# Eight of the 22 rows of blocks of a feed-forward's down product as seven products of sums, in the four feed-forwards of the second block

## The chip, the cores and the metric

The kernel runs on one core of a Trainium2 chip. The metric is the device time of one launch in microseconds; the median of three runs of the kernel before is 1603.33 us (1603.21 to 1605.09).

## The reference

Two transformer blocks over 256 tokens of width 1024, in float32. The first has a feed-forward, a mixer (neighbourhood attention and pooling), a second feed-forward and a gated embedding. The second block has six layers, and four of them are the feed-forwards that matter here:

```
def swiglu_2(x, w_in, w_out):
    gate, up = jnp.split(x @ w_in, 2, axis=-1)        # 1024 -> 2 x 2816
    return (jax.nn.silu(gate) * up) @ w_out           # 2816 -> 1024

for i in range(2):
    h = layer_norm(ALPHA * h + 0.5 * swiglu_2(h, ffn_w_in[i, 0], ffn_w_out[i, 0]), ...)
    h = layer_norm(ALPHA * h + mixer(h), ...)         # i = 0: gated linear attention, i = 1: retention
    h = layer_norm(ALPHA * h + 0.5 * swiglu_2(h, ffn_w_in[i, 1], ffn_w_out[i, 1]), ...)
```

Layer norms, attention and retention are unchanged by what follows, and so is the first block.

## The kernel before, in words

**Products.** All large products are done in a split form: each operand is a high part (rounded to the type fp32r) and a low part (the rest), and a product of blocks is three matmuls into the same PSUM bank, high by high, high by low, low by high (`mm3`, L215 to L219). The stationary operand is a block of 128 tokens by 128 rows of activations, the moving one 128 by 512 columns of weights. The 256 tokens are two token tiles.

**Weights** come in units of 128 x 2048 values (1 MB). `fetch` (L157) loads a unit into a `raw` buffer, ScalarE casts it to the high part `whi` (L174), and VectorE subtracts to get the low part `wlo` (L177). There are five buffers of each. The list `plan` holds the order of all units of the kernel; `unit` hands out the next one, and its argument `ahead` says how many units beyond it are to have been issued.

**Seven products for eight.** Where a weight matrix is taken as 2 x 2 blocks of 512 x 512 and the tokens as 2 x 2 blocks of 128 x 512, `seven` (L369) forms the four block products from seven products of sums (P1, P5, P7, P6, P3, P2, P4 in this order). Each has four block products (12 matmuls), a unit of weights of its own, made by `fetch_sum` (L182) from four raw units (L194 adds, L196 casts, L197 subtracts), and for P5, P7, P6 and P3 a sum of token blocks y1, y3, y2, y4, made by `sums_in` (L302). VectorE combines the results (L392 to L402). The kernel before does this for two of the six column chunks of gate and up in five feed-forwards, and for two pairs of chunks in the retention layer.

**A feed-forward** (`ffn`, L449) does the gate and up products chunk by chunk, multiplies silu(gate) by up (`finish`), transposes the result on TensorE and splits it into `hT[t, c]` for token tile t and chunk c. The down product (`lagged`, L406) then walks over 11 units of weights, each two rows of blocks (2 x 128 rows) by 1024 columns. For each unit `step(t, u)` does four block products (12 matmuls) into the two accumulators of token tile t; tile 1 follows tile 0 by three units, and the last two units of tile 1 are done one accumulator after the other. When tile 0 is finished, `after` adds it to the residual stream h and normalises it (`ln_post`, L329), and its transposes are put off by five and six ticks (`turn_in`); a tick is two block products. Tile 1's remaining steps run meanwhile.

**PSUM** buffers are eight, of one bank each: five with the tag `mm` (accumulators and products), three with the tag `tp` (transposes).

**Order.** The program is written as straight code with work put off by ticks (`defer`), but the order in each engine's queue is set when the kernel is built, by a list scheduler: of the instructions whose operands and buffers are expected to be there, the one written first goes first, and work written later is moved ahead if an engine would wait. Buffers of one tag are handed out in the order of the code. On the chip each queue then runs in the order written.

Of the kernel before, what the change touches and what calls it, by code (L numbers as in the profile page):

```python
# [11 lines left out]
F32 = mybir.dt.float32  # L12
# [20 lines left out]
LAG = 3  # L33
POOL_WINDOWS = (2, 4, 8, 16)
# [17 lines left out]
def ffn_units(g, u, d, seven=()):  # L52


    out = []
    for c in range(5):
        four = [(g, 2 * c), (g, 2 * c + 1), (u, 2 * c), (u, 2 * c + 1)]
        out += [(four, j) for j in range(7)] if c in seven else four
    return out + [(g, 10), (g, 11)] + [(d, i) for i in range(11)]
# [19 lines left out]
def all_units():  # L79
# [5 lines left out]
    p += ffn_units("s0g", "s0u", "s0d", SEVEN)  # L85
    p += chunk_units("gin", GLA_ORDER) + [("gout", i) for i in range(4)]
    p += ffn_units("s1g", "s1u", "s1d", SEVEN) + ffn_units("s2g", "s2u", "s2d", SEVEN)
    p += chunk_units("rin", RET_ORDER) + [("rout", i) for i in range(8)]
    return p + ffn_units("s3g", "s3u", "s3d", SEVEN)


class Build:
# [107 lines left out]
    def unit(self, name, i, kb, ahead=1):  # L200
# [3 lines left out]
        near = any(isinstance(p[0], list) for p in self.plan[self.taken:self.taken + 4])  # L204
# [200 lines left out]

    def lagged(self, x, name, n_units, after, lag=LAG, have=None, extra=None):  # L406


        lag = min(lag, n_units)
        late, self.late = self.late, None  # L410
        if late:
            self.defer(2, late)
# [18 lines left out]
        for i in range(n_units + lag):  # L431
            if i < n_units:
                w[i] = self.unit(name, i, 2, 0 if lag == n_units and i == lag - 1 else 1)
                step(0, i)
                if i == n_units - 1:
                    after(0, acc[0])
            if i >= lag and i - lag < n_units - 2:
                step(1, i - lag)
# [10 lines left out]
    def ffn(self, xT, r, wg, wu, wd, after, first=False, raws=None):  # L449
# [3 lines left out]
        def finish(c, t, ps_g, ps_u, n):  # L453
# [8 lines left out]
            if t == 0 and c:  # L462
                first_pr[c] = pr
            elif c:
                self.defer(4, lambda: turn(c, n, first_pr[c], pr))
            else:
                self.defer(4, lambda: hT.__setitem__((t, c), self.splitT(pr, n // P, "hT")))
# [15 lines left out]
        first_pr = {}  # L483

# [52 lines left out]
        self.lagged(lambda t, k: hT[t, k // 4][:, k % 4, :], wd, 11, after, have=lambda t, k: (t, k // 4) in hT)  # L537
# [471 lines left out]
    def run(self, ctx):  # L1009
# [89 lines left out]
        for i in range(6):  # L1099
            if i % 3 != 1:  # L1100
                f = 2 * (i // 3) + (i % 3) // 2
                body = lambda after: self.ffn(nx, None, f"s{f}g", f"s{f}u", f"s{f}d", after, raws=raws)
# [64 lines left out]
def layout(x, p, rpb, pool_w, pool_scale, w_in, w_br_attn, w_br_pool, w_out, ple_w_proj, ple_w_gate,  # L1167
# [21 lines left out]
    for i in range(2):  # L1189
        for j in range(2):  # L1190
            w = ffn_w_in_2[i, j]
            a[f"s{2 * i + j}g"], a[f"s{2 * i + j}u"] = units_ff(w[:, :DFF], w[:, DFF:])
            a[f"s{2 * i + j}d"] = units(ffn_w_out_2[i, j], 2, 1024)
# [27 lines left out]
```

## Time and profile before

| | |
|---|---|
| median of three runs | 1603.33 us |
| the profiled execution | 1602.33 us |
| its span, first to last instruction | 1600.5 us |
| TensorE busy | 1588.5 us, 99% |
| VectorE busy | 1189.7 us, 74% |
| ScalarE busy | 823.0 us, 51% |
| GpSimd busy | 102.5 us, 6% |
| granted TensorE clock, mean | 0.998 of full speed |
| moved by DMA | 308 MB, 192 GB/s |

The page groups instructions by line, engine, operation and operands; a row has their count, busy time, mean duration, and the idle time of the engine before them with what ended it. Matmuls are pipelined, so that one matmul's row shows 0.39 us, while the next one starts 0.23 us after it. In a timeline a line has the start in us from the span's start, the duration, engine, line of the kernel, operation, what it writes and reads, how many instructions were merged, and in brackets how long the engine stood idle before and what it waited for.

### The profile page before, as it was taken

To read this page: it belongs to the slowest core of one execution; us is meant where nothing else is said; L and a number is where in the kernel's file an instruction comes from. 1 tells how busy PE (TensorE), PEld (TensorE's weight loads), DVE (VectorE), ACT (ScalarE), POOL (GpSimd) and SP (SyncE) were. 2 spreads that over 40 slices of the span, in tenths; PEclk is the share of its full clock that TensorE was granted. 3 is DMA by queue.
4 is the path that set the end of the run, shared out by engine and by line. 5 is a ranking of instruction groups with operands and counts; after the bars stand their busy time and mean duration, and the time that the engine had idled before them with its cause. 6 is when DMAs were issued, how large, how long until landed. Compare 5 with 4: busy or idle time off the path is not lost. (4 is left out here: it accounts for less than half of the span.)

```text
span 1600.5 us, 18234 instructions
## 1 busy us (share of the span) xinstructions
PE 1588.5 (99%) x7377; PEld 1310.2 (82%) x7377; DVE 1189.7 (74%) x1050; ACT 823.0 (51%) x819; POOL 102.5 (6%) x102
## 2 busy tenths in 40 slices
PE   9999999999999999999999999999999999999998
PEld 7888888888888888888888888888888888888886
DVE  6654665568983789947648996699938899799954
ACT  7443554455562765634645553446624464456531
POOL 0000000000000100001012000100002401010000
PEclk9999999999999999999999999999999999999999
DMA  9764663543574555556534556545755543655550
GB/s 355 286 212 154 212 228 126 183 158 139 195 278 158 179 204 210 214 202 231 181 121 152 186 184 235 187 178 191 267 183 182 187 184 112 252 196 191 183 198 27
DMA packets 49796, 308.10 MB, mean 192 GB/s; under 512 B 6048, under 2 KB 7328, under 8 KB 15024
## 3 DMA queue, kind: packets, MB, share of 16 engines
q1 hardware_dynamic: 49568, 306.93, 53.1%
q8 instruction: 58, 0.95, 0.2%
q14 instruction: 26, 0.21, 0.0%
q10 hardware_dynamic: 144, 0.00, 0.0%
HBM read 305.86 MB, written 1.05 MB: 192 GB/s over the span
## 5 line engine op out<-in xcount | busy, mean ns | idle before, releaser
L177 DVE TENSOR_TENSOR wlo<-raw,whi 128x2048 fp32r<-128x2048 f32 (+1 forms) x239 | 520.2, 2184 | 273.8 <-ACT whi L174 273.8
L174 ACT CAST whi<-raw 128x2048 fp32r<-128x2048 f32 (+1 forms) x238 | 432.8, 1826 | 348.5 <-PE acc L219 190.5
L217 PE MATMUL mm<-whi,xTh 128*128 128x512 f32 x912 | 363.3, 398 | 0.2 <-ACT xTh L234 0.2
L219 PE MATMUL mm<-whi,xTl 128*128 128x512 f32 x912 | 356.3, 391 | 0.0
L218 PE MATMUL mm<-wlo,xTh 128*128 128x512 f32 x912 | 356.2, 391 | 0.0
L196 ACT CAST whi<-raw 128x2048 fp32r<-128x2048 f32 x84 | 160.3, 1910 | 104.7 <-DVE raw L194 66.7
L217 PE MATMUL acc<-whi,hTh 128*128 128x512 f32 x528 | 207.0, 392 | 0.0
L219 PE MATMUL acc<-whi,hTl 128*128 128x512 f32 x528 | 205.6, 389 | 0.0
L218 PE MATMUL acc<-wlo,hTh 128*128 128x512 f32 x528 | 205.5, 389 | 0.0
L219 PEld LDWEIGHTS mm<-whi,xTl 128*128 128x128 f32 x912 | 171.2, 188 | 37.7 <-DVE xTl L235 1.4
L217 PEld LDWEIGHTS mm<-whi,xTh 128*128 128x128 f32 x912 | 171.3, 188 | 35.7 <-issue 1.7
L218 PEld LDWEIGHTS mm<-wlo,xTh 128*128 128x128 f32 x912 | 171.5, 188 | 33.5
L197 DVE TENSOR_TENSOR wlo<-raw,whi 128x2048 fp32r<-128x2048 f32 x84 | 190.7, 2284 | 5.9 <-ACT whi L196 5.9
L219 PEld LDWEIGHTS acc<-whi,hTl 128*128 128x128 f32 x528 | 99.1, 188 | 21.0
L218 PEld LDWEIGHTS acc<-wlo,hTh 128*128 128x128 f32 x528 | 99.2, 188 | 20.1
L217 PEld LDWEIGHTS acc<-whi,hTh 128*128 128x128 f32 x528 | 99.1, 188 | 20.0
L194 DVE TENSOR_TENSOR raw<-raw 128x2048 f32<-128x2048 f32 x48 | 109.9, 2290 | 0.1
L217 PE MATMUL mm<-whi,xh 128*128 128x512 f32 x176 | 69.0, 394 | 0.7 <-ACT whi L174 0.4
L218 PE MATMUL mm<-wlo,xh 128*128 128x512 f32 x176 | 68.8, 391 | 0.0
L219 PE MATMUL mm<-whi,xl 128*128 128x512 f32 x176 | 68.6, 390 | 0.0
L234 ACT CAST hTh<-hT 128x512 fp32r<-128x512 f32 (+1 forms) x72 | 38.6, 546 | 56.0 <-PE hT L226 55.9
L341 POOL TENSOR_TENSOR rl<-mv,mhalf 128x1 f32<-128x1 f32 x12 | 11.7, 976 | 738.9 <-DVE mv L340 738.9
(259 smaller groups left out, 2027.4 us busy)
## 6 DMA issues: line engine op xcount, KB each, us to landing
raw<-in_rin SPq DMA_DIRECT2D x24, 1024.0 KB, 4.8
raw<-in_bin SPq DMA_DIRECT2D x16, 1024.0 KB, 4.8
raw<-in_f2g SPq DMA_DIRECT2D x12, 1024.0 KB, 4.8
raw<-in_s0g SPq DMA_DIRECT2D x12, 1024.0 KB, 4.7
raw<-in_gin SPq DMA_DIRECT2D x12, 1024.0 KB, 4.7
raw<-in_s1g SPq DMA_DIRECT2D x12, 1024.0 KB, 4.7
raw<-in_s2g SPq DMA_DIRECT2D x12, 1024.0 KB, 4.8
raw<-in_s3g SPq DMA_DIRECT2D x12, 1024.0 KB, 4.9
```

The lines of the kernel that those rows point to most:

```text
L174: nc.scalar.copy(hi[:, s], raw[:, s])
L177: nc.vector.tensor_tensor(out=lo[:, s], in0=raw[:, s], in1=hi[:, s].bitcast(F32), op=ALU.subtract)
L194: nc.vector.tensor_tensor(out=r[key], in0=r[key], in1=r[other], op=ALU.add)
L196: nc.scalar.copy(hi, r[key])
L197: nc.vector.tensor_tensor(out=lo, in0=r[key], in1=hi.bitcast(F32), op=ALU.subtract)
L217: mm(ps, x.hi, w.hi, start=start, stop=False)
L218: mm(ps, x.hi, w.lo, start=False, stop=False)
L219: mm(ps, x.lo, w.hi, start=False, stop=stop)
L234: self.nc.scalar.copy(hi, v)
L341: nc.gpsimd.tensor_tensor(out=r, in0=mv[:, 1:2], in1=self.mhalf[:, :1], op=ALU.pow)
```

## The change

In the four feed-forwards of the second block, the first eight rows of blocks of the down product (1024 x 1024 weights, chunks 0 and 1 of hT) are done as seven products of sums, the other 14 as before. A new list of units puts four of the ordinary units first (the lead, both token tiles at once), then the seven units of sums, then the remaining three. `seven_down` does the products: P6 in the fifth `mm` bank, the others in the three `tp` banks, since the accumulators hold four. Its combinations are not put together with the accumulators but added into h one by one (`into`). `pair_sums` makes the token sums: three blocks are put together again from high and low part and four differences formed on GpSimd, then split by ScalarE and VectorE; one block (`whole`) is kept unsplit. The loads of the next layer norm's gains, which use the buffers of y1 and y2, are issued after the seven products. On the host the first 1024 rows of the down weights are laid out as four 512 x 512 blocks.

```diff
--- before.py
+++ after.py
@@ -31,6 +31,7 @@
 ALPHA = 4 ** 0.25
 NEG = -3.0e38
 LAG = 3
+LEAD = 4
 POOL_WINDOWS = (2, 4, 8, 16)
 EDGE = 8
 SUMS = (("a", None), ("a", "b"), ("b", "c"), ("a", "c"), ("c", None), ("d", None), ("a", "d"))
@@ -49,14 +50,18 @@
         return Split(self.hi[i], self.lo[i])
 
 
-def ffn_units(g, u, d, seven=()):
+def ffn_units(g, u, d, seven=(), pair=False):
 
 
     out = []
     for c in range(5):
         four = [(g, 2 * c), (g, 2 * c + 1), (u, 2 * c), (u, 2 * c + 1)]
         out += [(four, j) for j in range(7)] if c in seven else four
-    return out + [(g, 10), (g, 11)] + [(d, i) for i in range(11)]
+    out += [(g, 10), (g, 11)]
+    if not pair:
+        return out + [(d, i) for i in range(11)]
+    return out + [(d, i) for i in range(4, 4 + LEAD)] + [([(d, i) for i in range(4)], j) for j in range(7)] + [(d, i) for i in range(4 + LEAD, 11)]
 
 
 def chunk_units(name, order):
@@ -82,11 +87,11 @@
     p += chunk_units("bin", MIX_ORDER) + [("bpl", 0), ("bat", 0), ("bpl", 1), ("bat", 1)] + [("bout", i) for i in range(4)]
     p += ffn_units("f2g", "f2u", "f2d", SEVEN)
     p += [("pgate", i) for i in range(4)] + [("pproj", 0)]
-    p += ffn_units("s0g", "s0u", "s0d", SEVEN)
+    p += ffn_units("s0g", "s0u", "s0d", SEVEN, True)
     p += chunk_units("gin", GLA_ORDER) + [("gout", i) for i in range(4)]
-    p += ffn_units("s1g", "s1u", "s1d", SEVEN) + ffn_units("s2g", "s2u", "s2d", SEVEN)
+    p += ffn_units("s1g", "s1u", "s1d", SEVEN, True) + ffn_units("s2g", "s2u", "s2d", SEVEN, True)
     p += chunk_units("rin", RET_ORDER) + [("rout", i) for i in range(8)]
-    return p + ffn_units("s3g", "s3u", "s3d", SEVEN)
+    return p + ffn_units("s3g", "s3u", "s3d", SEVEN, True)
 
 
 class Build:
@@ -201,7 +206,7 @@
 
         assert self.plan[self.taken] == (name, i), (name, i, self.plan[self.taken])
         self.taken += 1
-        near = any(isinstance(p[0], list) for p in self.plan[self.taken:self.taken + 4])
+        near = any(isinstance(p[0], list) and p[0][0][0][-1] != "d" for p in self.plan[self.taken:self.taken + 4])
         self.ahead(4 if near else ahead)
         w = self.ready[self.taken - 1]
         self.ready[self.taken - 1] = None
@@ -403,12 +408,53 @@
         done(1, u2, c22)
         yield
 
-    def lagged(self, x, name, n_units, after, lag=LAG, have=None, extra=None):
+    def seven_down(self, hT, y, four):
+        nc, TT = self.nc, self.nc.vector.tensor_tensor
+        def times(name, x, j):
+            ps = (self.M if name == "P6" else self.TP)(name)
+            w = self.unit(four, j, 4, 4)
+            for k in range(4):
+                self.mm3(ps, x[:, k, :], w[:, k, :], k == 0, k == 3)
+                if k % 2:
+                    self.tick()
+            return ps
+        def into(t, n, c):
+            h = self.h[t][:, n * CW:(n + 1) * CW]
+            nc.vector.scalar_tensor_tensor(out=h, in0=c, scalar=0.5, in1=h, op0=ALU.mult, op1=ALU.add)
+        t = lambda tag, name: self.T(tag, [P, CW], F32, name=name)
+        p1, u2, u4 = t("u", "p1"), t("u", "u2"), t("y", "u4")
+        nc.scalar.copy(p1, times("P1", hT[0, 0], 0))
+        self.settle(lambda: len(y) == 4)
+        p5 = times("P5", y[1], 1)
+        p7 = times("P7", y[3], 2)
+        TT(out=u2, in0=times("P6", y[2], 3), in1=p1, op=ALU.subtract)
+        TT(out=u4, in0=p5, in1=u2, op=ALU.add)
+        TT(out=u2, in0=u2, in1=p7, op=ALU.subtract)
+        self.defer(5, lambda: into(0, 1, u4))
+        p3 = times("P3", y[4], 4)
+        self.defer(1, lambda: into(0, 1, p3))
+        p2 = times("P2", hT[0, 1], 5)
+        TT(out=p1, in0=p2, in1=p1, op=ALU.add)
+        c22 = t("y", "c22")
+        TT(out=c22, in0=u4, in1=p7, op=ALU.subtract)
+        self.defer(4, lambda: into(0, 0, p1))
+        self.defer(6, lambda: into(1, 1, c22))
+        p4 = times("P4", hT[1, 1], 6)
+        TT(out=u2, in0=p4, in1=u2, op=ALU.subtract)
+        self.defer(4, lambda: into(1, 0, u2))
+    def lagged(self, x, name, n_units, after, lag=LAG, have=None, extra=None, lead=0, between=None):
 
 
         lag = min(lag, n_units)
+        u1 = 4 if between else 0
         late, self.late = self.late, None
-        if late:
+        if late and not between:
             self.defer(2, late)
         acc = {}
         w = {}
@@ -430,11 +476,16 @@
 
         for i in range(n_units + lag):
             if i < n_units:
-                w[i] = self.unit(name, i, 2, 0 if lag == n_units and i == lag - 1 else 1)
+                w[i] = self.unit(name, u1 + i, 2, 3 if i < lead else 0 if lag == n_units and i == lag - 1 else 1)
                 step(0, i)
+                if i < lead:
+                    step(1, i)
+                if between and i == lead - 1:
+                    between()
+                    self.defer(2, late)
                 if i == n_units - 1:
                     after(0, acc[0])
-            if i >= lag and i - lag < n_units - 2:
+            if lead <= i - lag < n_units - 2:
                 step(1, i - lag)
         u0 = n_units - 2
         if have:
@@ -446,7 +497,7 @@
                     self.tick()
         after(1, acc[1])
 
-    def ffn(self, xT, r, wg, wu, wd, after, first=False, raws=None):
+    def ffn(self, xT, r, wg, wu, wd, after, first=False, raws=None, pair=False):
         nc = self.nc
         hT = {}
 
@@ -464,7 +515,7 @@
             elif c:
                 self.defer(4, lambda: turn(c, n, first_pr[c], pr))
             else:
-                self.defer(4, lambda: hT.__setitem__((t, c), self.splitT(pr, n // P, "hT")))
+                self.defer(4, lambda: hT.__setitem__((t, c), whole(pr) if pair and t else self.splitT(pr, n // P, "hT")))
 
         def finish7(c):
             prs = []
@@ -481,6 +532,41 @@
             return done
 
         first_pr = {}
+        def whole(pr):
+            raw = self.S([P, CW], name="hr")
+            nc.scalar.copy(raw, self.transpose4(pr, 4, "hT"))
+            return raw
+        yh = {}
+        def pair_sums():
+            TT = nc.gpsimd.tensor_tensor
+            b4 = lambda v: v.rearrange("p (a b) -> p a b", a=4)
+            def raw(x, tag):
+                o = b4(self.T(tag, [P, CW], F32, name="hr"))
+                TT(out=o, in0=x.hi.bitcast(F32), in1=x.lo.bitcast(F32), op=ALU.add)
+                return o
+            def split(i, o):
+                if i < 3:
+                    both = self.T(("gp", "gq")[i - 1], [P, 2, 4, P], F32R, name="yT")
+                    hi, lo = both[:, 0], both[:, 1]
+                else:
+                    hi, lo = (b4(self.T("ld", [P, CW], F32R, name=n)) for n in ("yTh", "yTl"))
+                nc.scalar.copy(hi, o)
+                nc.vector.tensor_tensor(out=lo, in0=o, in1=hi.bitcast(F32), op=ALU.subtract)
+                yh[i] = Split(hi, lo)
+            a21 = b4(hT[1, 0])
+            a22 = raw(hT[1, 1], "u")
+            a11 = raw(hT[0, 0], "u")
+            a12 = raw(hT[0, 1], "y")
+            for n, (i, o, a, b) in enumerate(((1, a22, a21, a22), (3, a21, a11, a21), (2, a11, a11, a22), (4, a12, a12, a11))):
+                TT(out=o, in0=a, in1=b, op=ALU.subtract)
+                self.defer(6 + n, lambda i=i, o=o: split(i, o))
 
         def turn(c, n, *prs):
             tps = [self.transpose4(pr, n // P, "hT") for pr in prs]
@@ -534,7 +620,11 @@
                         finish(c, t, pss[t, nm][:, :256], pss[t, nm][:, 256:], 256)
                     elif nm == wu:
                         finish(c, t, pss[t, wg], pss[t, wu], CW)
-        self.lagged(lambda t, k: hT[t, k // 4][:, k % 4, :], wd, 11, after, have=lambda t, k: (t, k // 4) in hT)
+        if not pair:
+            return self.lagged(lambda t, k: hT[t, k // 4][:, k % 4, :], wd, 11, after, have=lambda t, k: (t, k // 4) in hT)
+        self.defer(1, pair_sums)
+        self.lagged(lambda t, k: hT[t, k // 4 + 2][:, k % 4, :], wd, 7, after, have=lambda t, k: (t, k // 4 + 2) in hT, lead=LEAD,
+                    between=lambda: self.seven_down(hT, yh, [(wd, i) for i in range(4)]))
 
     class Chunks:
 
@@ -1099,7 +1189,7 @@
         for i in range(6):
             if i % 3 != 1:
                 f = 2 * (i // 3) + (i % 3) // 2
-                body = lambda after: self.ffn(nx, None, f"s{f}g", f"s{f}u", f"s{f}d", after, raws=raws)
+                body = lambda after: self.ffn(nx, None, f"s{f}g", f"s{f}u", f"s{f}d", after, raws=raws, pair=True)
             elif i == 1:
                 body = lambda after: self.gla(nx, raws, after)
             else:
@@ -1190,7 +1280,8 @@
         for j in range(2):
             w = ffn_w_in_2[i, j]
             a[f"s{2 * i + j}g"], a[f"s{2 * i + j}u"] = units_ff(w[:, :DFF], w[:, DFF:])
-            a[f"s{2 * i + j}d"] = units(ffn_w_out_2[i, j], 2, 1024)
+            w = ffn_w_out_2[i, j]
+            a[f"s{2 * i + j}d"] = np.concatenate([units(w[:1024], 4, 512), units(w[1024:], 2, 1024)])
     for i in range(6):
         a[f"ln_g{i}"] = ln_g_2[i // 3, i % 3][None]
         a[f"ln_b{i}"] = ln_b_2[i // 3, i % 3][None]
```

## Rows read from the trace of the kernel before

**Rows 1.** Page, section 1: busy us, share of the span, instructions

```profile
PE 1588.5 (99%) x7377; PEld 1310.2 (82%) x7377; DVE 1189.7 (74%) x1050; ACT 823.0 (51%) x819; POOL 102.5 (6%) x102
```

**Rows 2.** Waits of TensorE (total us, times, longest), two of seven

```profile
PE spin L1030 <- POOL jk L1027: 1.3, 1, 1.3
...
PE mm L217 <- ACT xTh L234: 0.2, 1, 0.2
```

**Rows 3.** Timeline, TensorE, s0 (start us, duration, engine, line, operation, out<-in)

```profile
664.66 0.39 PE L217 MATMUL P<-whi,yTh 128*128 128x512 f32 x1
...
667.38 0.39 PE L217 MATMUL P<-whi,xTh 128*128 128x512 f32 x1
...
684.66 0.39 PE L217 MATMUL acc<-whi,hTh 128*128 128x512 f32 x1
...
685.34 0.39 PE L217 MATMUL acc<-whi,hTh 128*128 128x512 f32 x1
...
745.94 0.39 PE L217 MATMUL mm<-whi,xTh 128*128 128x512 f32 x1
```

**Rows 4.** Windows, three down stages (span; busy PE, PEld, DVE, ACT, POOL; clock)

```profile
684.66:745.94 61.28, 61.28 (x277) 50.73 (x276) 30.97 (x27) 22.27 (x17) 4.78 (x3) 1.00 0.52 182
976.38:1037.66 61.28, 61.28 (x277) 50.72 (x276) 30.96 (x27) 22.27 (x17) 4.84 (x3) 1.00 0.49 169
1157.63:1218.90 61.27, 61.27 (x277) 50.73 (x276) 30.95 (x27) 22.26 (x17) 4.83 (x3) 1.00 0.52 182
```

**Rows 5.** Timeline of VectorE, down products of s0

```profile
687.07 2.29 DVE L177 TENSOR_TENSOR wlo<-raw,whi 128x2048 fp32r<-128x2048 f32 x1 [0.59 <-ACT whi L174]
...
700.89 2.29 DVE L177 TENSOR_TENSOR wlo<-raw,whi 128x2048 fp32r<-128x2048 f32 x1 [9.21 <-ACT whi L174]
706.33 2.29 DVE L177 TENSOR_TENSOR wlo<-raw,whi 128x2048 fp32r<-128x2048 f32 x1 [3.15 <-ACT whi L174]
```

**Rows 6.** Timeline of ScalarE, up products of s0

```profile
667.62 1.92 ACT L174 CAST whi<-raw 128x2048 fp32r<-128x2048 f32 x1 [0.81 <-PE P L219]
```

**Rows 7.** Timeline of VectorE, up products of s0, behind P6

```profile
668.14 0.68 DVE L392 TENSOR_TENSOR u<-P,p 128x512 f32<-128x512 f32 x1
668.74 2.28 DVE L177 TENSOR_TENSOR wlo<-raw,whi 128x2048 fp32r<-128x2048 f32 x1
670.94 0.69 DVE L393 TENSOR_TENSOR u<-P,u 128x512 f32<-128x512 f32 x1
...
674.93 0.69 DVE L397 TENSOR_TENSOR u<-P,u 128x512 f32<-128x512 f32 x1
```

**Rows 8.** Timeline of TensorE, retention layer, second group of seven products

```profile
1361.86 0.39 PE L217 MATMUL P<-whi,xTh 128*128 128x512 f32 x1
1362.09 0.39 PE L217 MATMUL acc<-whi,gTh 128*128 128x512 f32 x1
1362.33 0.50 PE L218 MATMUL P<-wlo,xTh 128*128 128x512 f32 x1
```

**Rows 9.** Timeline of VectorE at the same place

```profile
1359.98 2.29 DVE L197 TENSOR_TENSOR wlo<-raw,whi 128x2048 fp32r<-128x2048 f32 x1
```

**Rows 10.** Timelines of GpSimd and VectorE, two-input operations, alone and together

```profile
796.79 1.48 POOL L797 TENSOR_TENSOR gate<-gate,gnorm 128x512 f32<-128x512 f32 x1 [39.08 <-ACT gate L796]
...
1255.87 0.74 POOL L943 TENSOR_TENSOR rot<-rb,ra 128x256 f32<-128x256 f32 x1
...
1257.72 2.78 POOL L943 TENSOR_TENSOR rot<-rb,ra 128x256 f32<-128x256 f32 x1
...
1257.08 2.83 DVE L177 TENSOR_TENSOR wlo<-raw,whi 128x2048 fp32r<-128x2048 f32 x1
```

**Rows 11.** Timeline of VectorE, end of s0's feed-forward

```profile
735.74 1.28 DVE L335 SCALAR_TENSOR_TENSOR h<-acc,h 128x512 f32<-128x512 f32 x2
...
743.42 0.69 DVE L235 TENSOR_TENSOR xTl<-xT,xTh 128x512 fp32r<-128x512 f32 x1
...
746.82 0.68 DVE L235 TENSOR_TENSOR xTl<-xT,xTh 128x512 fp32r<-128x512 f32 x1
```

## The prediction

> **What bounds the kernel now.** I read the engine shares first: TensorE is busy 99% of the span, VectorE 74%, GpSimd 6% [rows 1]. The list of TensorE's waits has seven rows, the longest 1.3 us [rows 2], so almost nothing is lost there: the time is TensorE's work. The timeline of TensorE in the first of the four feed-forwards concerned (s0) gives its rate. A block product is three matmuls, and the next begins 0.68 us later, 0.2267 us per matmul; the down products start at 684.66 and the next layer's first product at 745.94, 61.28 us for 264 matmuls (59.84 us) and three groups of transposes [rows 3]. The stages of the three feed-forwards with a layer behind them last 61.28, 61.28 and 61.27 us, with TensorE busy all the time and VectorE half of it [rows 4]; so I work out s0 and count it four times. In that stage VectorE sits idle for 9.21 us and then 3.15 us of every 5.44, waiting for a weight buffer [rows 5]. So there is room on VectorE exactly where the change puts work, and I ask whether it comes in time.
>
> **The change, part by part.** *Removed.* Per feed-forward 22 x 4 = 88 block products become 14 x 4 + 28 = 84. Four times 0.68 is 2.72 us, and four feed-forwards give 10.88 us of TensorE.
>
> *Added on VectorE, per feed-forward:* four sums of 2048 columns and three more low parts of weights (14 units where there were 11), 2.29 us each [rows 5], 16.0 us; four low parts of token sums, six combinations and five additions into h, 0.7 us each by the same operation in the up products [rows 7], 10.5 us; less one split that falls away. ScalarE gets three more casts of 1.91 us [rows 6]. All lie beside TensorE if they are in time, so I laid them out by hand for s0, on the clock of the trace. The lead (four units, both token tiles, 5.44 us each, one group of transposes) runs 684.66 to 706.77. The products P1, P5, P7, P6, P3, P2, P4 take 2.72 each; P6 ends at 717.65, P4 would end at 725.81.
>
> A unit's cast starts 0.24 us after the product that frees its buffer (667.38 to 667.62 [rows 3, 6]), takes 1.91, and its low part 2.29: ready about 4.45 us after. There are five buffers, so the sums for P6, P3, P2 and P4 get theirs at 701.3, 706.8, 709.5 and 712.2, are ready by 708.1, 712.6, 714.8 and 717.0 with VectorE's queue counted in, and are wanted at 714.9, 717.7, 720.4 and 723.1. VectorE is occupied about 27 of the 31 us up to P6's end. The weights are in time.
>
> *The narrow place is PSUM.* Four of the eight banks hold the accumulators, P6 takes a fifth, the other products share three. P2 needs the bank of P5, which is free after two combinations behind P6 (u2, u4); P4 needs that of P3, free when P3 has been added into h. In the up products these combinations queue behind weights: u2, a low part, u4, so that u4 starts at 670.94, 6.28 us after P6 ended at 664.66 [rows 7, 3]. By hand, here: the low part of unit 8 (8, 9 and 10 are the ordinary units that follow) ends 719.5, u2 720.1, unit 9's low part goes ahead of u4 (u4 must wait for u2's result), u4 ends 722.9; unit 10's low part, the rest of u2, P3 into h end at 726.3. P2 could start 2.6 us late, P4 another 0.7: 3.3 us if TensorE waits, more than the 2.72 gained.
>
> It need not wait. The order of each engine is chosen when the kernel is built, among what is expected to be ready. In the retention layer a product's second matmul had to wait for a low part that ended at 1362.27; a matmul of the following accumulation stands between the first (1361.86) and the second (1362.33), and no time is lost [rows 8, 9]. Here unit 8 is ready at 719.5, before P3 ends at 720.4; its 12 matmuls (2.72 us) fill P2's 2.6, and unit 9 fills P4's 0.7. I cost the bank waits at nothing, covered by these steps; without the cover they cost 3.3 us a feed-forward by hand, or 5.4 at the lags of rows 7 (u4 ends 6.97 after P6, so P2 starts 4.25 late; L397, in the place of P3 into h, ends 10.95 after P6, P4 another 1.2).
>
> *Token sums on GpSimd:* seven operations with two inputs of 512 columns. One took 1.48; one of 256 columns took 0.74 beside an operation that reads PSUM, and 2.78 beside a low part of weights, which itself took 2.83 instead of 2.29 [rows 10, 5]. Bounds: 7 x 1.48 = 10.4 us to 7 x 2 x 2.78 = 38.9 us per feed-forward. I take 3.8 us each (1.48 and a wait of one low part), 26.5 us; begun with the stage at 684.66 the last sum is there at 711.2 and split at 712.5, five before P3 wants it. At 38.9 it would be some 7 us late. VectorE's own loss is between nothing and the whole 10.4 us; I take 0.54 x 7 = 3.8, against 3 to 4 us of idle time before P6, and cost it at nothing. The trace thus shows both engines delayed when they overlap. The Trainium skill (SBUF — State Buffer, "Who interferes with whom") says that a VectorE instruction with two SBUF inputs and a GpSimd instruction that reads SBUF exclude each other for the whole instruction; by that rule VectorE would lose the whole of the bound just given, which is rival three; the row of the two that met shows 0.54 and so only a part of it.
>
> *Moved: the end of the stage.* Between tile 0's last product and the next layer's first, tile 1 had four steps (10.88 us) and now has three (8.16), with 0.71 us of transposes. Before: tile 0 ends at 745.94 - 11.59 = 734.35; its normalisation starts 1.39 later, behind a low part, and the low halves of the next input end at 744.11 and 747.50, 9.76 and 13.15 after [rows 11]. The next layer will want them at the third matmul of a product, 9.32 and 12.04 after. At unchanged offsets they are 0.44 and 1.11 late. So the bound above is 1.1 us for each of three layer ends (the fourth is followed by the output); the bound below is nothing, since the 1.39 need not recur and other products can go first. I take 0.5, 1.5 in all. Gains (ln_g, ln_b) wait for P5 and P6 now; the buffers are free 20 us before they are read, so nothing.
>
> **Sum.** The profiled execution took 1602.33 around a span of 1600.5; 1602.33 - 10.88 + 1.5 = 1592.95. The median of the runs is 1.0 higher, 1603.33, so the forecast is 1594.0. Its own range is 1592.0 (layer ends cost nothing, 1592.45, less 0.4 of scatter) to 1596.0 (1.1 each).
>
> **Rivals.**
> *One, the layer ends eat more.* VectorE enters the last steps with combinations and additions just finished (by hand 732.8, tile 0 ends at 734), and the chain is late by more than 1.1. The most is the step's 2.72, three times 8.16. For it: the 13.15 above is already late. Against: the weights that stood in that chain are prepared earlier now. Midway, 5.7 us lost: 1598.
>
> *Two, slower: the bank waits stay on TensorE.* If the order written into its queue is P3, P2, P4 without steps between, because the combinations are expected sooner than VectorE gives them, TensorE stands 3.3 to 5.4 us in each feed-forward. It decides from 2.72. For it: rows 7. Against: rows 8 and 2, where such orders hardly ever cost anything. Net 0.6 to 2.7 us, four times: 1605.7 to 1614; midway 1610.
>
> *Three, GpSimd and VectorE hold each other up.* If VectorE loses most of 10.4 us, sums and unit 8 come late and nothing is ready to fill with. Loss 0 to about 5 us a feed-forward; at 2.72 the gain is gone: 1603.
>
> **Chances.** Forecast 0.62, one 0.16, two 0.12, three 0.10. A measurement can tell 0.2% (3.2 us), so faster means below 1600.1 and slower above 1606.5. Faster: 0.62, 0.155 of one, 0.015 of three: 0.79. Same: about 0.005 of one, 0.02 of two and 0.06 of three, 0.08 with rounding. Slower: 0.10 of two and 0.025 of three, 0.13. The range, 1591.8 to 1602.0, takes the forecast's own with 0.2 for scatter, nearly all of one, and three up to a gain of a tenth of the 10.88; it leaves out two.
>
> **What would show it.** Right: 7329 matmuls instead of 7377; in each of the four stages a group of accumulating matmuls between P3 and P2 and between P2 and P4; TensorE's list of waits about as short as before; GpSimd some 42 to 106 us busier (4 x 10.4 to 4 x 26.5); each stage 2.2 to 2.7 us shorter from its first matmul to the next layer's first. Wrong: TensorE waiting on the combinations or on h at the products P2 and P4 (rival two), on xT at a layer's first products (one), on low parts of weights or token sums in the seven products (three).

## The result, and the profile after

The changed kernel takes 1628.48 us (median of four runs, 1628.32 to 1628.71) against 1603.34 for the kernel before: 1.0153 times as long, 95% interval 1.0141 to 1.0166. It is slower by 25 us where 9 us of gain were forecast. The profiled execution has a span of 1626.6 us, 26.1 more than before.

Section 1 of the page after answers to [rows 1]: 48 matmuls fewer, as intended, VectorE 99 us busier, GpSimd 54 us.

```profile
PE 1589.8 (98%) x7329; PEld 1306.5 (80%) x7329; DVE 1288.7 (79%) x1134; ACT 855.3 (53%) x851; POOL 156.7 (10%) x130
```

TensorE's waits, which were next to nothing [rows 2] (columns: total us, times, longest us):

```profile
PE hT L231 <- DVE pr L527: 16.4, 4, 4.1
PE P L222 <- DVE u L435: 3.3, 4, 0.8
PE acc L223 <- DVE wlo L182: 3.3, 4, 1.3
...
PE mm L222 <- ACT xTh L239: 0.9, 4, 0.2
```

The first three stand there four times, once per feed-forward; of the four on xTh three are new, at the ends of the first three feed-forwards, and one is that of [rows 2]. The long one is not in the down products: it is the transposes of chunk 4, the last up products, waiting for the product pr of silu and up. The timeline of ScalarE at that place in s0 shows why.

```profile
677.28 0.63 ACT L526 ACTIVATE sg<-p 128x512 f32<-128x512 f32 x1 [1.36 <-DVE p L404]
684.52 0.62 ACT L559 CAST yT<-hr 128x512 fp32r<-128x512 f32 x1 [6.61 <-POOL hr L568]
685.04 1.89 ACT L179 CAST whi<-raw 128x2048 fp32r<-128x2048 f32 x1
686.84 0.63 ACT L526 ACTIVATE sg<-u 128x512 f32<-128x512 f32 x1
```

The second silu of chunk 4 (L526) stands in ScalarE's queue behind the cast of the first token sum (L559), and that cast waits 6.61 us for GpSimd; the cast of a unit of weights (L179) stands between the two, as it stood ahead of the silu before. The timeline of GpSimd: the sums begin at 678.00, not with the down products (what they waited for last is the silu at 677.28, which reads the buffer that the first of them writes), and the first two take 3.2 us each.

```profile
678.00 3.19 POOL L550 TENSOR_TENSOR hr<-hTh,hTl 128x512 f32<-128x512 f32 x1 [99.16 <-ACT sg L526]
681.27 3.22 POOL L568 TENSOR_TENSOR hr<-hr 128x512 f32<-128x512 f32 x1
684.44 1.27 POOL L550 TENSOR_TENSOR hr<-hTh,hTl 128x512 f32<-128x512 f32 x1
```

VectorE had the silu's input (L407) ready at 680.65; it did one low part of weights and then sat idle 4.16 us, until the silu was done. Before, that silu ran at 680.31 (first row, ScalarE in the kernel before; then VectorE after).

```profile
680.31 0.63 ACT L475 ACTIVATE sg<-u 128x512 f32<-128x512 f32 x1
679.96 0.69 DVE L407 TENSOR_TENSOR u<-P,u 128x512 f32<-128x512 f32 x1
680.56 2.78 DVE L182 TENSOR_TENSOR wlo<-raw,whi 128x2048 fp32r<-128x2048 f32 x1
687.50 0.69 DVE L527 TENSOR_TENSOR pr<-c,sg 128x512 f32<-128x512 f32 x1 [4.16 <-ACT sg L526]
```

TensorE stands from 684.05 to 688.34, and then goes slowly: its matmuls begin 0.43 us apart until 693.49, and 0.23 after.

```profile
683.82 0.39 PE L222 MATMUL mm<-whi,xTh 128*128 128x512 f32 x1
688.34 1.09 PE L231 MATMUL hT<-ident,pr 128*128 128x128 f32 x4 [4.14 <-DVE pr L527]
...
690.08 0.63 PE L222 MATMUL mm<-whi,xTh 128*128 128x512 f32 x1
690.51 0.63 PE L223 MATMUL mm<-wlo,xTh 128*128 128x512 f32 x1
...
693.87 0.39 PE L222 MATMUL acc<-whi,hTh 128*128 128x512 f32 x1
```

Windows over the 10 us behind the wait and the next 10 (the third column from the end is the granted clock): 0.73 behind the wait, thus partly at the lower of the two levels (1.2 and 2.4 GHz), after TensorE had done nothing for 4.3 us; from 688.34 to 693.49 alone it is 0.50.

```profile
688.34:698.35 10.01, 10.01 (x37) 8.20 (x38) 5.29 (x6) 4.32 (x6) 6.77 (x4) 0.73 0.32 113
698.35:708.35 10.00, 10.00 (x47) 8.30 (x46) 10.00 (x10) 3.84 (x4) 0.00 (x0) 1.00 0.00 0
```

The sum for s0, from the first product of chunk 4's seven to the next layer's first matmul: 93.08 us before (652.86 to 745.94), 99.31 after (653.88 to 753.19). The 6.23 are the pause of 4.29, some 2.5 of slow matmuls, 0.5 and 1.0 at the two waits of the down stage, 0.5 at the layer end and some 0.2 of rest, less the 2.72 that were removed. Four times 6.23 is 25 (the fourth feed-forward has no layer behind it).

### The profile page after: what moved, and what is told of

Same layout as the page of the kernel before. It is cut to its first block, busy times and chain, and to the rows that moved or that the text cites. A ratio compares the mean times of both kernels' runs of the same rounds, so it can differ in the third digit from the quotient of the medians.

```text
span 1626.6 us, 18302 instructions
## 1 busy us (share of the span) xinstructions
PE 1589.8 (98%) x7329; PEld 1306.5 (80%) x7329; DVE 1288.7 (79%) x1134; ACT 855.3 (53%) x851; POOL 156.7 (10%) x130
## 5 line engine op out<-in xcount | busy, mean ns | idle before, releaser
L182 DVE TENSOR_TENSOR wlo<-raw,whi 128x2048 fp32r<-128x2048 f32 (+1 forms) x223 | 487.5, 2193 | 163.4 <-ACT whi L179 163.2
L179 ACT CAST whi<-raw 128x2048 fp32r<-128x2048 f32 (+1 forms) x222 | 403.0, 1821 | 271.4 <-PE acc L224 98.9
L201 ACT CAST whi<-raw 128x2048 fp32r<-128x2048 f32 x112 | 213.4, 1909 | 151.5 <-DVE raw L199 101.3
L202 DVE TENSOR_TENSOR wlo<-raw,whi 128x2048 fp32r<-128x2048 f32 x112 | 253.9, 2285 | 23.0 <-ACT whi L201 23.0
L223 PE MATMUL acc<-wlo,hTh 128*128 128x512 f32 x400 | 158.1, 395 | 3.3 <-DVE wlo L182 3.3
L222 PE MATMUL acc<-whi,hTh 128*128 128x512 f32 x400 | 158.8, 397 | 0.0
L224 PE MATMUL acc<-whi,hTl 128*128 128x512 f32 x400 | 157.2, 393 | 0.0
L199 DVE TENSOR_TENSOR raw<-raw 128x2048 f32<-128x2048 f32 x64 | 146.6, 2291 | 0.4
L550 POOL TENSOR_TENSOR hr<-hTh,hTl 128x512 f32<-128x512 f32 x12 | 25.0, 2080 | 410.0 <-ACT sg L526 410.0
L240 DVE TENSOR_TENSOR hTl<-hT,hTh 128x512 fp32r<-128x512 f32 (+1 forms) x68 | 42.7, 638 | 18.5 <-ACT hTh L239 18.3
```

What stands on the lines that cost most here:

```text
L179: nc.scalar.copy(hi[:, s], raw[:, s])
L182: nc.vector.tensor_tensor(out=lo[:, s], in0=raw[:, s], in1=hi[:, s].bitcast(F32), op=ALU.subtract)
L199: nc.vector.tensor_tensor(out=r[key], in0=r[key], in1=r[other], op=ALU.add)
L201: nc.scalar.copy(hi, r[key])
L202: nc.vector.tensor_tensor(out=lo, in0=r[key], in1=hi.bitcast(F32), op=ALU.subtract)
L222: mm(ps, x.hi, w.hi, start=start, stop=False)
```

## Experiments

Three theories were on record. A: ScalarE is caught behind a cast whose sum GpSimd delivers late. B: GpSimd lengthens VectorE's instructions wherever they meet. C: the new order of the down stage is at fault. Each diff shows the main lines of its edit.

**The token sums by VectorE.**

```diff
-            TT = nc.gpsimd.tensor_tensor
+            TT = nc.vector.tensor_tensor
```

> The seven token sums of each of the four feed-forwards run on VectorE instead of GpSimd; nothing else is changed. Theory A (ScalarE is caught behind a token sum that GpSimd delivers late: the cast of y1 stands in its queue ahead of the second silu of chunk 4, TensorE waits 4.1 us for that silu's product and then runs 2.5 us slower at the lower clock, in each feed-forward): the sums take 0.7 us each, the wait and the slow stretch go, 1628.5 - 4 x 6.75 = 1601.5, between 1599 and 1604, no wait of TensorE for pr above 0.5 us. Theory B (GpSimd holds VectorE itself through the shared SBUF port, so that weights and sums come late; the place of the cast does not matter): the same time here, about 1601. Theory C (the new order of the down stage, lead, PSUM banks and bank waits, is what costs; the wait for pr is only where it shows): 1626 to 1630.

1607.28 us, ratio 1.0023 (1.0014 to 1.0033), above the 1599 to 1604 that A named, and far below C's. The wait for pr is gone, and with it 21 of the 25 us. What is left moved: the order now has P2 right behind P3 and P4 27 accumulating matmuls later, and the layer end comes late (columns as above).

```profile
PE mm L222 <- ACT xTh L239: 4.2, 4, 1.3
PE mm L223 <- DVE wlo L182: 1.4, 3, 0.5
```

TensorE's matmuls, counted from the front, place the loss. Against the kernel without sums (third experiment) the profiled execution is 12.8 us longer. The stretch from chunk 4's seven products to the next layer's first matmul takes 2.25 us more in each of the three feed-forwards with a layer behind them, and 0.4 in the fourth; the 12 us behind the three layer ends take another 2.6, 1.1 and 1.2. So some 10 of the 12.8 us are lost at the layer ends.

**The casts of the sums behind chunk 5's casts in ScalarE's queue.** `self.c5` is the last cast of chunk 5's transposed tiles.

```diff
-                nc.scalar.copy(hi, o)
+                with self.tc.issue_after(self.c5):
+                    nc.scalar.copy(hi, o)
```

> Token sums stay on GpSimd; the four casts of the token sums are placed in ScalarE's queue behind the cast of chunk 5's activations, by an ordering edge alone. Theory A: GpSimd is as slow as before, but nobody waits for it; the wait for pr and the slow clock go, 1599 to 1604, GpSimd's seven sums still some 2 to 3 us each in the mean. Theory B: GpSimd still overlaps the same work of VectorE, so the time stays above 1620. Theory C: 1626 to 1630.

1608.02 us, ratio 1.0027 (1.0018 to 1.0037). One edge in one queue gives 20 us back: A has the bulk, though the time is above the 1599 to 1604 that it named; B's "above 1620" and C are out. What stays are three waits:

```profile
PE hT L231 <- DVE pr L527: 3.8, 4, 0.9
PE P L222 <- DVE u L435: 3.3, 4, 0.8
PE acc L223 <- DVE wlo L182: 3.3, 4, 0.9
```

The first is B's: on VectorE's timeline the low part in front of pr takes 2.80 instead of 2.29 us and pr itself 1.77 instead of 0.69, while GpSimd is at a sum.

```profile
680.55 2.80 DVE L182 TENSOR_TENSOR wlo<-raw,whi 128x2048 fp32r<-128x2048 f32 x1
683.27 1.77 DVE L527 TENSOR_TENSOR pr<-c,sg 128x512 f32<-128x512 f32 x1
```

**No token sums.** Products 5, 6, 7 and 3 take tiles that are already there, so they multiply other operands; sums, their casts and their low parts are left out.

```diff
+            yh.update({1: hT[1, 0], 2: hT[1, 1], 3: hT[0, 0], 4: hT[0, 1]})
...
-            for n, (i, o, a, b) in enumerate(((1, a22, a21, a22), (3, a21, a11, a21), (2, a11, a11, a22), (4, a12, a12, a11))):
```

> The token sums are left out altogether: unsplit blocks of hT stand in for y1 to y4, so the seven products multiply other operands and the output is not the reference's; the sums of weights, the products, combinations and additions into h are all there. This is the price of the down stage's new order without any sums. Theory A and B: 1599 to 1602. Theory C: above 1615.

1595.33 us, ratio 0.9947 (0.9931 to 0.9964), below the 1599 to 1602 that A and B named, and 1.3 us above the 1594.0 of the prediction. The rest of the change does what was forecast for it. So the price of the token sums in the changed kernel is 33 us (1628.48 - 1595.33), more than the 25 of the net loss. The stretch that took 93.08 us takes 90.84 (window over s0):

```profile
653.04:743.88 90.84, 90.63 (x414) 74.71 (x412) 85.28 (x69) 49.90 (x37) 2.56 (x3) 1.00 0.62 229
```

**The sums alone, in the kernel before.** The sums, casts and low parts run; nobody reads them, the down products are the old ones.

```diff
+        if pair:
+            self.defer(1, pair_sums)
...
-            self.defer(2, late)
+            self.defer(14 if name[0] == 's' else 2, late)
```

> The kernel before, plus the seven token sums on GpSimd and their four splits alone, whose results nothing reads (the gains' loads are issued 12 ticks later, since they share the buffers); products, units and weights as before. Theory A: y1's cast stands at the same place of ScalarE's queue, so the whole loss is here: 1603.3 + 4 x 6.75 = 1630, between 1624 and 1634, with TensorE waiting about 4 us for pr four times. Theory B: some of it, 1608 to 1625, without the wait for pr. Theory C: 1602 to 1606.

1628.06 us, ratio 1.015 (1.0135 to 1.0165): 25 us lost without any new product, by the same wait. C falls as the cause of it. That the time equals the changed kernel's is partly chance: here nothing is gained, and the waits of the down stage (3.3 and 3.3 us) are missing, some 8 of the 33 us.

```profile
PE hT L226 <- DVE pr L476: 16.4, 4, 4.1
```

**The sums behind chunk 4.** On top of the edge of the second experiment, the three tiles lie in buffers that chunk 5 frees. The queues of TensorE, VectorE and ScalarE keep their order; in GpSimd's, the third block is put together behind three of the differences instead of ahead of them.

```diff
-            a22 = raw(hT[1, 1], "u")
-            a11 = raw(hT[0, 0], "u")
-            a12 = raw(hT[0, 1], "y")
+            a22 = raw(hT[1, 1], "sg")
+            a11 = raw(hT[0, 0], "sg")
+            a12 = raw(hT[0, 1], "sg")
```

> Order of instructions as in the kernel with y1's cast behind chunk 5 (1608.0 us), but the three token tiles lie in the buffers that chunk 5's silus and products leave, so GpSimd can begin only about 686 us into the profile instead of 678, behind chunk 4's combinations. B (GpSimd lengthens VectorE's instructions wherever they meet, 4.4 us in each FFN, and VectorE has some 5 us of slack in front of the down products): the transposes of chunk 4 no longer wait for pr (0.95 us per FFN, 3.8 in all), but the lengthening moves on to the down stage, where low parts and u4 come as late or later; 1602 to 1607. E (it is only the meeting with chunk 4's combinations that costs): all waits go, 1596 to 1599. D (the work itself, four low parts of 0.69 us per FFN, is too much for VectorE): the two waits of the down stage stay as they are, 1603 to 1605.

1617.93 us, ratio 1.0086 (1.0071 to 1.0101), 10 us more than with the early start and outside every range. Chunk 4's wait is gone, but a larger one stands in the down stage:

```profile
PE acc L223 <- DVE wlo L182: 14.3, 4, 3.6
```

VectorE's timeline ahead of it: two low parts of sums at 1.78 instead of 0.68, a low part of weights at 3.37.

```profile
699.71 1.77 DVE L561 TENSOR_TENSOR yT<-hr,yT 128x512 fp32r<-128x512 f32 x1
701.40 1.78 DVE L561 TENSOR_TENSOR yTl<-hr,yTh 128x512 fp32r<-128x512 f32 x1
703.10 3.37 DVE L202 TENSOR_TENSOR wlo<-raw,whi 128x2048 fp32r<-128x2048 f32 x1
```

In s0 no instruction of VectorE waits for a sum's cast in this stretch, so it is the lengthening that makes it late, not the sums' arrival. The wait is long enough to bring the slow clock back (last section): the list of waits is only some 4 us longer than in the second experiment (14.3 against 10.4 for its three), the time 10.

**Casts and low parts without GpSimd's sums.** The four splits read chunk 0's second token tile as it is; GpSimd's seven instructions are left out.

```diff
-                TT(out=o, in0=a, in1=b, op=ALU.subtract)
-                self.defer(6 + n, lambda i=i, o=o: split(i, o))
+            for i in (1, 3, 2, 4):
+                self.defer((6, 8, 7, 9)[i - 1], lambda i=i: split(i, a21))
```

> GpSimd's seven instructions are left out; the four casts and the four low parts stay and read chunk 0's second token tile as it is, so products 3, 5, 6 and 7 have other operands and the output is not the reference's. B: without GpSimd VectorE's instructions have their lengths again, the four low parts (2.7 us per FFN) fit into the 4.5 us that VectorE idled without any sums; 1595 to 1598, no wait for wlo or u4. D: 1602 to 1606 with waits acc<-wlo and P<-u as before.

1595.46 us, ratio 0.9945 (0.993 to 0.996), with none of the waits: the casts and low parts are free.

**P5 copied out of PSUM by ScalarE**, on top of the fifth.

```diff
-        p5 = times("P5", y[1], 1)
+        p5 = t("sg", "p5")
+        nc.scalar.copy(p5, times("P5", y[1], 1))
```

> As e5, and ScalarE copies P5 out of PSUM, so P2's bank no longer waits for u4 on VectorE; the order of the down stage becomes P3, P2, 15 accumulating matmuls, P4. B: P2 waits no more (0.8 us and the gap behind it, some 1 us per FFN), acc's wait for a low part may stay; 1598 to 1603, thus at or below the kernel before. If VectorE's lateness as such sets the stage, the wait turns up at P4 or at the weights behind it and the time stays that of e5 within 1 us.

1620.11 us, ratio 1.01 (1.0085 to 1.0115). The wait turned up at the next place, P4's bank, as its second case said; the time is that of the fifth within the intervals, though not within the 1 us named. Freeing P2's bank gained nothing while VectorE as a whole was late; on acc's low parts 3.5 us of waits are left.

```profile
PE P L222 <- DVE h L426: 13.1, 4, 3.3
```

**GpSimd's sums without casts and low parts**, placed as in the fifth, read by nobody; the products take the tiles of the third.

```diff
-                self.defer(6 + n, lambda i=i, o=o: split(i, o))
+            yh.update({1: hT[1, 0], 2: hT[1, 1], 3: hT[0, 0], 4: hT[0, 1]})
```

> GpSimd's seven instructions run as in e5, but nobody reads them: no casts and no low parts of sums, the products take the operands of the kernel without sums (output not the reference's). B: VectorE loses 3 to 4.4 us per FFN to lengthened instructions, less than or about its idle time of 4.5; 1595 to 1601, with VectorE's instructions beside GpSimd's at 1.7 and 2.7 to 3.3 us instead of 0.69 and 2.29. D: 1595 to 1596, as without sums. If e6 and e8 both come near 1595 and e5 does not, it is the sum of the two that passes VectorE's slack.

1597.03 us, ratio 0.9957 (0.994 to 0.9973). Each half alone costs 0 to 2 us, both together 22. The busy times of VectorE say what adds up. Section 1 of the pages, in this order: no sums, casts and low parts only, GpSimd's sums only, both:

```profile
PE 1579.2 (99%) x7329; PEld 1301.1 (82%) x7329; DVE 1279.3 (80%) x1122; ACT 847.8 (53%) x835; POOL 97.9 (6%) x102
```

```profile
PE 1579.0 (99%) x7329; PEld 1301.2 (82%) x7329; DVE 1285.6 (81%) x1134; ACT 857.0 (54%) x851; POOL 95.6 (6%) x102
```

```profile
PE 1579.7 (99%) x7329; PEld 1301.6 (82%) x7329; DVE 1298.8 (81%) x1122; ACT 849.5 (53%) x835; POOL 179.1 (11%) x130
```

```profile
PE 1589.1 (98%) x7329; PEld 1307.9 (81%) x7329; DVE 1307.4 (81%) x1134; ACT 856.7 (53%) x851; POOL 166.2 (10%) x130
```

With the same number of instructions of its own, VectorE is 19.5 us busier for GpSimd's sums alone (1298.8 - 1279.3, 4.9 per feed-forward) and 21.8 beside the low parts (1307.4 - 1285.6, 5.45). The four low parts are 2.4, 0.6 from one to the next. Without sums VectorE idled 0.58, 2.33, 0.83, 0.91 and 0.43 us between 687 and 720 in s0, 5.1 in all; 4.9 or 2.4 go into that, 7.9 do not, the less so as 2.6 of the idle time stay idle in the fifth experiment too (0.60 and 2.03 before low parts that wait for ScalarE's cast).

**The sums in chunks 2 and 3.** Same seven GpSimd instructions, 40 us earlier, with tiles of their own and three instructions of one column that hold them at their places; the casts find them ready.

```diff
+                if pair and c == 2:
+                    early(c, t, pr)
...
+                o = self.S([P, CW], name="hr")
+                nc.gpsimd.tensor_scalar(out=o[:, :1], in0=pr[:, :1], scalar1=1.0, scalar2=0.0, op0=ALU.mult, op1=ALU.add)
```

> The whole change, output the reference's. GpSimd's seven instructions run some 60 to 80 us earlier, behind chunk 2's two products and chunk 3's first, into tiles of the pool S; the casts stand behind chunk 5's as in e6 and find their sums ready. If what made e5 slow (1617.9) is that casts and low parts meet with sums that are late and with a VectorE that GpSimd lengthens at the same time, as e6 (1595.5) and e8 (1597.0) say together, the down stage runs as in e6 and the lengthening of some 5 us per FFN falls where VectorE is busy 17.5 of 20 us (600 to 620) and 18.2 of 20 (640 to 660): 1595 to 1600, faster than before. If VectorE has no slack there either, the loss shows as waits of chunk 3's or 4's transposes for pr or of matmuls for wlo, up to 5 us per FFN: 1600 to 1615.

1613.67 us, ratio 1.0055 (1.0041 to 1.0069), in the second range. The down stage has no wait left, so late sums are not needed for a loss; the 23.2 us by which VectorE is busier than in the sixth experiment (1308.8 - 1285.6) now make chunk 2's transposes and chunk 4's products wait.

```profile
PE P L222 <- DVE u L397: 6.6, 4, 1.7
PE hT L231 <- DVE pr L529: 6.5, 4, 1.7
```

**The sums by VectorE, in its idle stretches.** Two in chunk 1, two between chunk 3's products, three behind the sum of weights for P6 in the down stage, pinned there by edges in its queue.

```diff
+                with self.tc.issue_after(self.raw3):
+                    rw[4] = raw(hT[0, 1])
+                    TT(out=rw[2], in0=rw[2], in1=rw[1], op=ALU.subtract)
+                    TT(out=rw[4], in0=rw[4], in1=rw[2], op=ALU.subtract)
```

> The whole change, output the reference's. No GpSimd: VectorE makes the seven sums itself, 0.60 us each from one to the next, 4.2 us per FFN, against some 5.4 us by which GpSimd's seven lengthened it in e5 and e9. Two stand in chunk 1 (0.4 us before a stretch where VectorE idled 1.75 us for ScalarE's cast in e6), two between chunk 3's two products (1.80 us idle in e6), three in the down stage between a sum of weights and its low part (2.03 us idle in e6). B' (each GpSimd sum takes VectorE's time as much as a sum made by VectorE does, and what counts is whether it meets idle time of VectorE): all seven fit, 1595 to 1599, faster than before. If it is GpSimd's lateness and not VectorE's time that cost in e5 and e9, or if the idle time is not there when two queues shift, waits stay: 1600 to 1608.

1595.98 us, ratio 0.9953 (0.9939 to 0.9966): the whole computation, 7.5 us below the kernel before and within 1 us of leaving the sums out, with no wait left in the down stage. Section 1 and the three sums in the down stage, where the kernel with casts and low parts only idled 2.03 us:

```profile
PE 1580.5 (99%) x7329; PEld 1301.8 (82%) x7329; DVE 1302.7 (82%) x1162; ACT 855.0 (54%) x851; POOL 97.9 (6%) x102
```

```profile
704.02 0.68 DVE L553 TENSOR_TENSOR hr<-hTh,hTl 128x512 f32<-128x512 f32 x1
704.63 0.68 DVE L565 TENSOR_TENSOR hr<-hr 128x512 f32<-128x512 f32 x1
705.34 0.69 DVE L566 TENSOR_TENSOR hr<-hr 128x512 f32<-128x512 f32 x1
706.14 2.29 DVE L204 TENSOR_TENSOR wlo<-raw,whi 128x2048 fp32r<-128x2048 f32 x1
```

VectorE's own 28 sums took 17.1 us (1302.7 - 1285.6); for GpSimd's 28 it lost 21.8 and 23.2.

**GpSimd's sums at about these places.**

```diff
-            TT = nc.vector.tensor_tensor
+            TT = nc.gpsimd.tensor_tensor
...
-                early(1)
+                early(1, pr)
```

> As the kernel with VectorE's sums in its idle stretches (1596.0), but GpSimd makes the seven sums again, at about the same places: two in chunk 1, three from the first product of chunk 3 on, two from the sum of weights in the down stage on; casts and low parts are where they were. If the place alone decides, 1596 to 1599. If each GpSimd sum takes 0.7 to 0.8 us from VectorE and runs 3.2 us where VectorE works, longer than the idle stretches of 1.5 to 2 us, part of the waits comes back (hT or P behind combinations, acc behind a low part): 1599 to 1606, and VectorE's busy time some 3 to 6 us above the 1302.7 of the kernel compared with.

1604.33 us, ratio 1.0002 (0.9993 to 1.0012), in the second range. Better placed, GpSimd's sums cost 8 us more than VectorE's. VectorE's busy time was expected above 1302.7 and is 1300.7, below that of VectorE's own sums, so its busy time is not what cost the 8 us here. The sums that fall into idle time take 1.3 us and nothing from VectorE. One that outlasts it runs into the low parts behind (GpSimd's timeline):

```profile
653.41 1.30 POOL L565 TENSOR_TENSOR hr<-hr 128x512 f32<-128x512 f32 x1
654.79 3.23 POOL L568 TENSOR_TENSOR hr<-hr 128x512 f32<-128x512 f32 x1
```

In the down stage the last sum meets a low part, which keeps its 2.29; the sum itself comes late, ScalarE waits 3.51 us at its cast, and VectorE 1.84 us behind that. TensorE's longest wait, 0.8 us for u4 at P2, stands behind it, 3.1 of the 5.5 us of new waits in its list.

```profile
706.43 3.36 POOL L569 TENSOR_TENSOR hr<-hr 128x512 f32<-128x512 f32 x1
709.83 0.62 ACT L580 CAST yTh<-hr 128x512 fp32r<-128x512 f32 x1 [3.51 <-POOL hr L569]
710.48 0.69 DVE L581 TENSOR_TENSOR yTl<-hr,yTh 128x512 fp32r<-128x512 f32 x1 [1.84 <-ACT yTh L580]
```

## Why the prediction was wrong

The step that failed is "token sums on GpSimd", costed at nothing: it asked whether the last sum reaches its product in time, not what stands behind the first sum's cast in ScalarE's queue. The runs showed a wait of 4.1 us there and 2.5 us of slow matmuls behind it, in each feed-forward. Point by point:

- *Removed, 10.88 us.* Right: 7329 matmuls. Without the sums the kernel gained 8.0 us, with well-placed sums 7.5; the layer ends (three times some 0.45) account for 1.4 of the rest to 10.88, and some 1.5 stay unexplained.
- *VectorE's weights in time, PSUM's narrow place filled.* Right. Accumulating matmuls stand between P3 and P2 and between P2 and P4 (11 and 4 in s0), and without sums or with VectorE's in its gaps nothing waits there. Rival two's sign is there, but small: TensorE waits 0.8 us for u4 at P2, and up to 1.3 for a low part. Both waits go when the sums go and the order stays, so the order alone is not their cause.
- *Layer ends, 0.5 each.* Right: the next layer's first matmul comes 0.8 us behind the last transposes, a wait of 0.2 us on xTh at each of the three and some 0.45 lost.
- *Token sums.* "Begun with the stage at 684.66" was an assumption; they began at 678.00, because their buffers were free then, among chunk 4's combinations, and the last was there at 695.34, 16 us before the 711.2 worked out. "Five before P3 wants it" asked for the last sum alone. What decided was the first sum's cast: ScalarE takes its queue in order, and the order had that cast ahead of chunk 4's second silu. The prediction named no instruction queued behind the waiting cast, on ScalarE, and so missed a wait of 4.1 us and the slow clock that followed, together 6.8 us of the 8.95 (6.23 + 2.72) lost per feed-forward. One edge in that queue recovered 20 us; the sums alone in the kernel before lost 25.
- *"3.8 us each" and "0.54 x 7 = 3.8".* GpSimd's time was overestimated: its seven sums took 15.2 us per feed-forward (3.2 at the most, 1.3 alone) and not 26.5. VectorE's loss was misjudged: the 0.54 of [rows 10] is no price of a meeting, but what was left of GpSimd's operation when VectorE's began (last section). In the changed kernel VectorE lost only 0.8 per feed-forward (1288.7 against 1285.6 with the same instructions and no sums), because it stood idle for ScalarE meanwhile; this term is not what made the 25 us. Where VectorE had work, it lost 3.8 to 5.8. The idle time was about right: 3.1 us are left between 687 and 720 in s0 beside casts and low parts alone (sixth experiment), so that the loss could not be free there.
- *Rival three* had the two engines right and their price too low (1603), since it, too, looked only at unit 8 and the sums' arrival. Most of the loss is not its mechanism, but ScalarE's queue; with the cast out of the way its mechanism gave 1608 to 1618.

What stays open: the 1.5 us between the gain without sums and what was removed; why the profiled kernel with VectorE's sums, placed by the scheduler, runs slowly for a while behind its first layer end (granted clock 0.71 from 747.05 to 753.00) after waits of no more than 1.3 us each; and whether GpSimd's sums, cut so as to fit idle stretches, would equal VectorE's.

## What to carry to other kernels

When work is moved to an idle engine, look at the first consumer of its first result: what stands behind that consumer in its in-order queue, and what it costs if the result comes late. Moving a two-input operation from VectorE to GpSimd saved VectorE little or nothing here while both read SBUF: 28 sums cost VectorE 17 us when it made them and 15 to 23 when GpSimd did and VectorE had other work, and even at 15 the kernel was 8 us slower. Idle time counts once: add up everything that is to go into it, and put short instructions where the gaps are.

## What the runs showed of the hardware

Instructions of GpSimd and VectorE that both have two inputs in SBUF took turns, each for its whole length. GpSimd's sum of 512 columns takes 1.26 to 1.30 us alone and 3.2 beside low parts of weights; VectorE's instructions take 1.77 instead of 0.69 and 3.37 instead of 2.29, each 1.08 more. GpSimd's two sums at the place of the three VectorE rows of the fifth experiment:

```profile
700.89 1.74 POOL L550 TENSOR_TENSOR hr<-hTh,hTl 128x512 f32<-128x512 f32 x1
702.71 1.62 POOL L569 TENSOR_TENSOR hr<-hr 128x512 f32<-128x512 f32 x1
```

The sum of 700.89 ends at 702.63, 1.15 us after VectorE's low part of 699.71 (701.48); the next low part, begun at 701.40, ends 0.55 after that sum (703.18); the next sum ends 1.15 after this low part (704.33); and the low part of 3.37 ends 2.14 after that (706.47). So each waited for the other's end. In the changed kernel and experiments two, five, eight, nine and eleven, 128 of the 136 VectorE instructions of 512 or 2048 columns with both inputs in SBUF that began during one of these sums were longer by what was left of the sum, less 0.13 to 0.14 us; beside the other 8 the sum was itself still waiting, and they kept their length. That is why some are longer by 1.08 and others by 0.5. The 40 with an input in PSUM kept theirs within 0.02 us. Of the 168 sums 124 began during such an instruction of VectorE; 116 of them ended 1.12 to 1.17 us after it.

The prediction had weighed the rule of the Trainium skill (SBUF — State Buffer, "Who interferes with whom"), by which the two exclude each other for the whole instruction, against one row with 0.54, and sided with the row. These runs agree with the rule, and so does that row. The kernel before has this operation of GpSimd ahead of the one of 2.78 us in [rows 10]:

```profile
1256.65 1.10 POOL L942 TENSOR_TENSOR rot<-ra,rb 128x256 f32<-128x256 f32 x1
```

It ends at 1257.75, 0.67 us after the low part began (1257.08); less 0.13 that is the 0.54.

After a pause of 4.3 us TensorE's matmuls came 0.43 us apart for some 5 us and cost 2.5 us more; after one of 3.7 in the fifth experiment (it ends at 727.59) the granted clock was 0.61 over the 4.3 us from 727.24 on (window):

```profile
727.24:731.58 4.34, 3.99 (x11) 3.13 (x12) 4.34 (x5) 0.43 (x1) 0.00 (x0) 0.61 1.02 340
```

So waits of 4.1 and 3.6 us in the list cost some 6.8 and 5.1 here (the second an estimate: 11 matmuls in 3.99 us behind it, where 0.23 each would make 2.5), about one and a half times what the list shows.
